# A two-layer decoder trunk in split fp32: new SBUF addresses for h's transpose, the operand sums and the activations

## The chip, the cores and the metric

The kernel runs on one core of one Trainium2 chip. The metric is device time in microseconds (us) of one execution; times of single instructions are in nanoseconds (ns). TensorE does the matrix products (PE in the profile, with PEld for its weight loads), VectorE is DVE, ScalarE is ACT, GpSimd is POOL, and SyncE (SP) issues the DMAs.

## The reference, cut to what matters

Two layers over 512 tokens of width 1024; layer 0 mixes with gated linear attention (GLA), layer 1 with retention. All of it is float32.

```python
for i in range(DEPTH):                       # DEPTH = 2
    h = layer_norm(DN_ALPHA * h + 0.5 * swiglu(h, ffn_w_in[i, 0], ffn_w_out[i, 0]), ...)
    m = gla_mixer(h, ...) if i == 0 else retention_mixer(h, ...)
    h = layer_norm(DN_ALPHA * h + m, ...)
    h = layer_norm(DN_ALPHA * h + 0.5 * swiglu(h, ffn_w_in[i, 1], ffn_w_out[i, 1]), ...)

def swiglu(x, w_in, w_out):                  # 1024 -> 2 x 2816 -> 1024
    gate, up = jnp.split(x @ w_in, 2, axis=-1)
    return (jax.nn.silu(gate) * up) @ w_out
```

## The kernel before

Every float32 operand of a large product is split into a rounded part (`hi`) and the rest (`lo`), both of type fp32r, and one product becomes three matmuls, hi·hi, hi·lo and lo·hi, in `mm3` (L151, L152, L153). A matmul has a *stationary* operand of 128 x 128, which TensorE loads beforehand (LDWEIGHTS, a row of PEld), and a *moving* operand of 256 or 512 columns, which is streamed past it. In the profile's names of matmuls, `out<-a,b`, the moving operand is `a` and the stationary one is `b`: `po<-whi,ahi` streams the weights `whi` past the activation `ahi`.

Weights arrive by DMA in granules of 128 x 2048 floats (`wf`), and ACT and DVE split them into `whi` and `wlo` (L105, L106) ahead of their use. The stages and the roles of the operands are:

- **Feature-major projections** (`fm`): the stationary operand is a block of weights, the moving one is h's transpose `hThi`/`hTlo`, 512 or 256 columns wide.
- **The FFN's first product** (`products`, in `seven_products`): seven half-size products instead of eight. Three of them stream a quarter of hT (`p1`, `a12`, `a22`), four stream a sum of quarters of hT (`Shi`/`Slo`, made once for each FFN in `operand_sums`), each 256 columns wide, with 4 x 3 matmuls to a product. The weights are stationary.
- **The FFN's second product** (`po<-whi,ahi` and so on): a 128-column slice of an activation `ahi`/`alo` is stationary, and 512 columns of weights are streamed. The ten activation buffers of each kind are used in turn.
- **Token-major projections** (`pvr` in GLA, `pv` and `pgg` in retention): a slice of hT is stationary, 512 columns of weights are streamed.
- **The mixers' output product** (`po<-whi,yhi`): a slice of the mixer's result `yhi`/`ylo` is stationary, 512 columns of weights are streamed.

Where a tile lies in SBUF is decided by the order of allocation: each pool is a stack of its tags, one after the other in each partition, each with its size in bytes. `cpool` (h, hT, `ident`, `mhalf`, `wgl`) comes first, then `wpool` (`wf`, `whi`, `wlo`), and above it the pool of the stage (`ffn..`, `gla`, `ret`). Almost all tiles are multiples of 256 bytes long in a partition, so that what stands before a pool decides the address of all of its tiles mod 256. Every slice that a matmul reads begins a multiple of 512 bytes into its tile. So each operand has one address mod 256, whatever the slice:

| operand | mod 256, before |
|---|---|
| `hThi`, `hTlo` | 128 |
| `whi`, `wlo` | 192 |
| `Shi0..3`, `Slo0..3` | 192 |
| `ahi`, `alo` (all) | 192 |
| `yhi`, `ylo` in GLA | 192 |
| `yhi`, `ylo` in retention | 0 |

Of each matmul the text looks at one number, the *distance*: the address of the stationary operand that is loaded for the next matmul, less the address of the moving operand of this matmul, mod 256.

Of the kernel before, what the change touches and what calls it, by code (L numbers as in the profile page):

```python
# [10 lines left out]
F32 = mybir.dt.float32  # L11
F32R = mybir.dt.float32r
# [5 lines left out]
P = 128  # L18
T = 512
# [5 lines left out]
NFC = 10  # L25
# [13 lines left out]
def _ffn_plan():  # L39

    plan = []
    for c, (f0, f1) in enumerate(CHUNKS):
        n = 0
        for f in range(f0, f1):
            plan.append(("in", f))
            if c and (f - f0) % 2 == 0 and n < (CHUNKS[c - 1][1] - CHUNKS[c - 1][0]) // 2:
                plan.append(("out", c - 1, n))
                n += 1  # L50
    return plan + [("out", len(CHUNKS) - 1, i) for i in range((CHUNKS[-1][1] - CHUNKS[-1][0]) // 2)]
# [14 lines left out]
def tile_decoder(ctx: ExitStack, tc: tile.TileContext, a: dict, out: bass.AP):  # L66
    nc = tc.nc
# [3 lines left out]
    cpool = ctx.enter_context(tc.tile_pool(name="cpool", bufs=1))  # L71
# [5 lines left out]
    class Stream:  # L77
# [59 lines left out]
        def next(self):  # L137
            i = self.at
            self.at += 1
            self.prepare(i)  # L140
            self.load(i + 1)
            self.prepare(i + 1)
            self.load(i + 2)
            return self.split[i]
# [10 lines left out]
    def pick(pair, *idx):  # L155
        return tuple(x[idx] for x in pair)
# [4 lines left out]
    def new_hT():  # L161
        hT[0] = tuple(
            cpool.tile([P, KD, T], F32R, tag=f"hT{s}", name=f"hT{s}")
            for s in ("hi", "lo")
        )
        return hT[0]
# [3 lines left out]
    with tc.tile_pool(name="start", bufs=1) as sp:  # L170
        hi, lo = new_hT()
# [13 lines left out]

    ident = cpool.tile([P, P], F32, name="ident")
    make_identity(nc, ident)
    mhalf = cpool.tile([P, 16], F32, name="mhalf")
    nc.gpsimd.memset(mhalf, -0.5)

    wgl = cpool.tile([P, KD, GRANK], F32, name="wgl")
# [1 line left out]
    def load_h():  # L193
        for t in range(NT):
            nc.sync.dma_start(h[t], a["x"][t * P:(t + 1) * P, :])


    def load_gb(tp, n, tags=("ln_g", "ln_b")):
        gb = []
        for name, tag in zip(("ln_g", "ln_b"), tags):  # L200
            x = tp.tile([P, D], F32, tag=tag, name=f"{name}{n}", bufs=1)
            nc.sync.dma_start(x, a[name][n].partition_broadcast(P))
            gb.append(x)
        return gb
# [32 lines left out]
    def feature_major(w, ranges, ps=None):  # L237

        w = [tuple(x.rearrange("p (k c) -> p k c", k=4) for x in b) for b in w]
        ps = ps or [pacc.tile([P, T], F32, tag="acc", name="fm") for _ in range(2)]  # L240
        for j in range(2):
            for r in ranges:
                for k in range(KD):
                    mm3(ps[j][:, r], pick(w[j if k < 4 else 3 - j], slice(None), k % 4),
                        pick(hT[0], slice(None), k, r), k == 0, k == KD - 1)
        return ps

    WHOLE = [slice(0, T)]
    H = T // 2
# [3 lines left out]
    def two_granules_ahead():  # L253


        g = [ws.next(), ws.next()]
        ps = [[pacc.tile([P, T], F32, tag="acc", name="fm") for _ in range(2)] for _ in g]
        for r in HALVES:
            for w, p in zip(g, ps):
                feature_major(w, [r], p)  # L260
        return ps
# [32 lines left out]
    def out_steps(lhs, n, first, halves=(0, 1), tp=None):  # L294


        for half in halves:
            ps = [pacc.tile([P, 512], F32, tag="acc", name="po") for _ in range(NT)]
            for k in range(n):
                def step(r):  # L300
                    for t in range(NT):
                        mm3(ps[t], lhs(k, t), r, k == 0, k == n - 1)
                        if k == n - 1:
                            add_out(t, half, ps[t], first, tp)
                yield step

    def out_by_halves(lhs, n, units, half, first, tp):
        for k, step in enumerate(out_steps(lhs, n, first, [half], tp)):
            step(units[half * n + k])
# [47 lines left out]

    def operand_sums(tp):

        s = [tuple(tp.tile([P, 4, H], F32R, tag=f"S{c}{i}", name=f"S{c}{i}", bufs=1) for c in ("hi", "lo")) for i in range(4)]  # L360
        for c in range(2):
            def full(k, ts, tag):
                x = tp.tile([P, 2, H], F32, tag=tag, name="hsum")
                nc.vector.tensor_add(x, *(y.bitcast(F32) for y in pick(hT[0], slice(None), slice(k + 2 * c, k + 2 * c + 2), ts)))
                return x

            def parts(x, i):
                hi, lo = pick(s[i], slice(None), slice(2 * c, 2 * c + 2))
                nc.scalar.copy(hi, x)
                nc.vector.tensor_sub(lo, x, hi.bitcast(F32))  # L370

            x21 = full(0, HALVES[1], "gate")
            s1 = full(4, HALVES[1], "up")
            nc.vector.tensor_add(s1, s1, x21)
            parts(s1, 0)
            x11 = full(0, HALVES[0], "gate")
            nc.vector.tensor_sub(x21, x11, x21)
            parts(x21, 2)
            nc.vector.tensor_sub(x11, s1, x11)
            parts(x11, 1)  # L380
            x12 = full(4, HALVES[0], "up")
            nc.vector.tensor_sub(x12, x12, x11)
            parts(x12, 3)
        return s

    def ffn(layer, which, ln, last=False, first=False):
        with tc.tile_pool(name=f"ffn{layer}{which}", bufs=2) as tp:
            ws.sums_pool = tp
            act = {}

            def activate(f, gate, up):
                sg = tp.tile([P, T], F32, tag="gate", name="sg")
                nc.scalar.activation(sg, gate, AF.Silu)
                nc.vector.scalar_tensor_tensor(out=sg, in0=sg, scalar=0.5, in1=up, op0=ALU.mult, op1=ALU.mult)
                hi = tp.tile([P, T], F32R, tag="ahi", name="ahi", bufs=NFC)
                lo = tp.tile([P, T], F32R, tag="alo", name="alo", bufs=NFC)
                nc.scalar.copy(hi, sg)
                nc.vector.tensor_sub(lo, sg, hi.bitcast(F32))
                act[f] = (hi, lo)

            def lhs(k0):
                return lambda k, t: tuple(x[:, t * P:(t + 1) * P] for x in act[k0 + k])

            if first:
                for f in range(2):
                    activate(f, *feature_major(ws.next(), WHOLE))
                load_h()
                nc.sync.dma_start(wgl, a["gla_w_low"].rearrange("(k p) c -> p k c", p=P))
            else:
                for f, ps in enumerate(two_granules_ahead()):  # L410
                    activate(f, *ps)
            s = operand_sums(tp)
            outs = {}
            for what, n, *i in _ffn_plan()[2:]:
                f0, f1 = CHUNKS[-1 if what == "in" else n]
                if what == "in":
                    activate(n, *(seven_products(ws.next(), s, tp) if n in FAST else feature_major(ws.next(), WHOLE)))
                elif f1 < NF:
                    if n not in outs:
                        outs[n] = out_steps(lhs(f0), f1 - f0, n == 0)  # L420
                    for u in ws.next():
                        next(outs[n])(u)
            f0, f1 = CHUNKS[-1]
            gb = load_gb(tp, ln, ("Shi0", "Slo0"))
            if not last:
                new_hT()
            def place(j):
                return lambda: tuple(tp.tile([P, 2 * B], F32R, tag=f"S{c}{j}", name=f"w{c}", bufs=1) for c in ("hi", "lo"))

            for j in range(3):  # L430
                ws.place[ws.at + (3 + j) // 2, (3 + j) % 2] = place(1 + j)
            units = Units()
            if not last:
                out_by_halves(lhs(f0), f1 - f0, units, 0, False, tp)
                for i in range(3):
                    ws.prepare(ws.at + i)
            out_by_tokens(lhs(f0), f1 - f0, units, [0, 1] if last else [1], False,
                          lambda t: layer_norm(tp, t, gb, last), tp)
# [200 lines left out]
    def retention(ln):  # L639
        with tc.tile_pool(name="ret", bufs=1) as tp:  # L640
            cos = tp.tile([P, T], F32, name="cos")
            sin = tp.tile([P, T], F32, name="sin")
            gcol = tp.tile([P, 16], F32, name="rgcol")
            for x, n in ((cos, "cos"), (sin, "sin"), (gcol[:, :RDV // P], "ret_norm_g")):
                nc.sync.dma_start(x, a[n])

# [74 lines left out]
            for hd in range(RH):  # L721
# [3 lines left out]
                S = scores(hd, q, k)  # L725
# [13 lines left out]
    ffn(0, 1, 2)  # L739
    ffn(1, 0, 3)  # L740
    retention(4)
    ffn(1, 1, 5, last=True)

# [89 lines left out]
```

## Time and profile before

| | |
|---|---|
| time, median of 3 runs | 2032.46 us (2031.47 to 2032.55) |
| profiled execution, its time | 2032.29 us |
| its span, first to last instruction | 2030.2 us |
| PE busy | 2015.7 us, 99% |
| PEld busy | 1796.5 us, 88% |
| DVE busy | 1515.6 us, 75% |
| ACT busy | 797.2 us, 39% |
| granted TensorE clock | 0.999 |

The busy time of an engine is the union of its instructions' times. A matmul's recorded time reaches beyond the start of the next one, so the *pace*, from one start to the next, is read from the start times. The profiled execution's time is 2.1 us above its span.

### The profile page before, as it was taken

The numbers are of one execution on the slowest core, as the hardware profiler recorded it, in microseconds if no ns is written. First come the engines' busy times: TensorE is split into PE (matmuls) and PEld (weight loads), VectorE is DVE, ScalarE is ACT, GpSimd is POOL, SyncE is SP. The second block draws the span as 40 slices with busy tenths as digits, with TensorE's granted clock in tenths as the row PEclk, the third lists the DMA queues.
The fourth block names the chain that finished last, engine by engine and source line by source line (L and its number), as shares of the span: only waits on it lengthen the run. The fifth ranks groups of instructions, "written<-read, shape, count | busy, mean of one in ns | idle before, by whom it ended". The sixth has DMA issues, their size and how long they took to land.

```text
span 2030.2 us, 29592 instructions
## 1 busy us (share of the span) xinstructions
PE 2015.7 (99%) x12364; PEld 1796.5 (88%) x12364; DVE 1515.6 (75%) x2152; ACT 797.2 (39%) x1131; POOL 37.2 (2%) x56
## 2 busy tenths in 40 slices
PE   8999999999999999999999999999999999999998
PEld 7999998888889999998999998888888878999997
DVE  7888888745588888888888888554545468888886
ACT  5444433632234344443444433333232324443441
POOL 0000000000000000000000000000000000000000
PEclk9999999999999999999999999999999999999999
DMA  6322223112222222341332223222222213322322
GB/s 212 122 104 104 104 95 134 66 66 80 104 83 104 104 104 104 104 146 43 125 104 104 104 88 141 104 76 99 74 91 74 91 69 104 119 91 103 110 98 83
DMA packets 33637, 205.00 MB, mean 101 GB/s; under 512 B 5056, under 2 KB 5184, under 8 KB 10592
## 3 DMA queue, kind: packets, MB, share of 16 engines
q1 hardware_dynamic: 33504, 203.12, 28.2%
q8 instruction: 97, 1.59, 0.3%
q14 instruction: 36, 0.29, 0.0%
HBM read 201.00 MB, written 2.10 MB: 100 GB/s over the span
## 4 chain that ended last, share of the span: by engine, by line
PE 97%; DVE 1%; ACT 1%; DMA 1%; issue 0%; SPq 0%; DVEq 0%; ACTq 0%
PE products L151 12%; PE products L153 12%; PE products L152 12%; PE po L151 10%; PE po L152 10%; PE po L153 10%; PE fm L153 5%; PE fm L151 5%; PE fm L152 5%; PE pv L152 1%; PE pgg L153 1%; PE pv L153 1%; PE pv L151 1%; PE pgg L152 1%; PE pgg L151 1%; PE pvr L153 1%
## 5 line engine op out<-in xcount | busy, mean ns | idle before, releaser
L106 DVE TENSOR_TENSOR wlo<-wf,whi 128x512 fp32r<-128x512 f32 (+1 forms) x362 | 399.4, 1107 | 95.8 <-ACT whi L105 94.3
L105 ACT CAST whi<-wf 128x512 fp32r<-128x512 f32 (+1 forms) x362 | 346.1, 959 | 296.2 <-PE po L153 130.3
L153 PE MATMUL products<-Shi,wlo 128*128 128x256 f32 x1152 | 325.6, 283 | 0.0
L151 PE MATMUL products<-Shi,whi 128*128 128x256 f32 x1152 | 325.5, 283 | 0.0
L152 PE MATMUL products<-Slo,whi 128*128 128x256 f32 x1152 | 324.8, 282 | 0.0
L151 PE MATMUL po<-whi,ahi 128*128 128x512 f32 x704 | 274.9, 391 | 0.0
L152 PE MATMUL po<-wlo,ahi 128*128 128x512 f32 x704 | 274.6, 390 | 0.0
L153 PE MATMUL po<-whi,alo 128*128 128x512 f32 x704 | 274.1, 390 | 0.0
L151 PE MATMUL products<-hThi,whi 128*128 128x256 f32 x864 | 241.1, 279 | 0.0
L152 PE MATMUL products<-hTlo,whi 128*128 128x256 f32 x864 | 240.6, 278 | 0.0
L153 PE MATMUL products<-hThi,wlo 128*128 128x256 f32 x864 | 240.2, 278 | 0.0
L151 PEld LDWEIGHTS products<-Shi,whi 128*128 128x128 f32 x1152 | 219.7, 191 | 0.4
L153 PEld LDWEIGHTS products<-Shi,wlo 128*128 128x128 f32 x1152 | 219.8, 191 | 0.0
L152 PEld LDWEIGHTS products<-Slo,whi 128*128 128x128 f32 x1152 | 219.7, 191 | 0.0
L105 ACT CAST whi<-sums 128x1024 fp32r<-128x1024 f32 x144 | 150.4, 1047 | 158.5 <-DVE h L277 70.1
L151 PE MATMUL fm<-hThi,whi 128*128 128x512 f32 (+1 forms) x592 | 202.0, 341 | 5.1 <-ACT hThi L183 5.1
L152 PE MATMUL fm<-hTlo,whi 128*128 128x512 f32 (+1 forms) x592 | 202.1, 341 | 0.0
L153 PE MATMUL fm<-hThi,wlo 128*128 128x512 f32 (+1 forms) x592 | 201.7, 341 | 0.1
L106 DVE TENSOR_TENSOR wlo<-sums,whi 128x1024 fp32r<-128x1024 f32 x144 | 175.6, 1222 | 24.3 <-ACT whi L105 24.3
L152 PEld LDWEIGHTS products<-hTlo,whi 128*128 128x128 f32 x864 | 162.7, 188 | 1.4
L151 PEld LDWEIGHTS products<-hThi,whi 128*128 128x128 f32 x864 | 162.7, 188 | 1.4
L153 PEld LDWEIGHTS products<-hThi,wlo 128*128 128x128 f32 x864 | 163.5, 189 | 0.0
(185 smaller groups left out, 3423.7 us busy)
## 6 DMA issues: line engine op xcount, KB each, us to landing
wf<-in_wts SPq DMA_DIRECT2D x179, 1024.0 KB, 4.8
ln_b<-in_ln_b SPq DMA_DIRECT2D x6, 512.0 KB, 3.5
ln_g<-in_ln_g SPq DMA_DIRECT2D x6, 512.0 KB, 5.2
xs<-in_xT SPq DMA_DIRECT2D x8, 256.0 KB, 5.3
h<-in_x SPq DMA_DIRECT2D x4, 512.0 KB, 8.1
out_h<-h SPq DMA_DIRECT2D x8, 256.0 KB, 2.0
wf<-in_wts SPq DMA_DIRECT2D x4, 256.0 KB, 5.6
dm<-in_decay SPq DMA_DIRECT2D x4, 256.0 KB, 3.1
```

The source lines that it names most:

```text
L105: nc.scalar.copy(hi, src)
L106: nc.vector.tensor_sub(lo, src, hi.bitcast(F32))
L151: nc.tensor.matmul(ps, l[0], r[0], start=start, stop=False)
L152: nc.tensor.matmul(ps, l[0], r[1], start=False, stop=False)
L153: nc.tensor.matmul(ps, l[1], r[0], start=False, stop=stop)
```

## The change

No instruction is added, taken away or moved on any engine: all five streams hold the same operations on the same tiles in the same order with the same waits. Only the tiles' addresses differ.

```diff
-    mhalf = cpool.tile([P, 16], F32, name="mhalf")
+    mhalf = cpool.tile([P, 32], F32, name="mhalf")
...
-        s = [tuple(tp.tile([P, 4, H], F32R, tag=f"S{c}{i}", name=f"S{c}{i}", bufs=1) for c in ("hi", "lo")) for i in range(4)]
+        s = []
+        for i, n in enumerate((16, 16, 16, 40)):
+            tp.tile([P, n], F32, tag=f"gap{i}", name="gap", bufs=1)
+            s.append(tuple(tp.tile([P, 4, H], F32R, tag=f"S{c}{i}", name=f"S{c}{i}", bufs=1) for c in ("hi", "lo")))
...
-                hi = tp.tile([P, T], F32R, tag="ahi", name="ahi", bufs=NFC)
-                lo = tp.tile([P, T], F32R, tag="alo", name="alo", bufs=NFC)
+                hi, lo = (tp.tile([P, T + 16], F32R, tag=f"a{c}", name=f"a{c}", bufs=NFC)[:, :T] for c in ("hi", "lo"))
...
-            gcol = tp.tile([P, 16], F32, name="rgcol")
+            gcol = tp.tile([P, 64], F32, name="rgcol")
...
-    nc = bacc.Bacc("TRN2", target_bir_lowering=False, num_devices=1)
+    nc = bacc.Bacc("TRN2", target_bir_lowering=False, num_devices=1, dynamic_dma_scratch_size=1024)
```

The last edit frees 15,360 bytes (60 x 256) of each partition at its bottom, which the longer tiles need; it moves everything by a multiple of 256. `mhalf` is 64 bytes longer, so the weights move by 64 against h and hT. Unused tiles of 64, 64, 64 and 160 bytes stand before the four pairs of operand sums. Each activation buffer is 64 bytes longer, so the ten buffers of a kind lie at 0, 64, 128, 192, 0, ... `rgcol` is 192 bytes longer, so what follows it in retention's pool lies at 0 as the weights now do.

The distances, as defined above, with the number of matmuls that have them (fp32r alone; a matmul at the joint of two stages can differ from its group):

| moving, then stationary | columns | matmuls | before | after |
|---|---|---|---|---|
| S, then weights (`products`) | 256 | 3456 | 0 | 192, 128, 64 and 160 for S0, S1, S2 and S3 |
| hT, then weights (`products`, `fm`) | 256 | 3456 | 64 | 128 |
| hT, then weights (`fm`) | 512 | 912 | 64 | 128 |
| weights, then hT (`pvr`, `pv`, `pgg`) | 512 | 1152 | 192 | 128 |
| weights, then activations (`po`) | 512 | 2112 | 0 | 0 for some 541, 64 for 543, 128 for 429, 192 for 460, others for the rest |
| weights, then retention's y (`po`) | 512 | 384 | 64 | 0 |
| weights, then GLA's y (`po`) | 512 | 192 | 0 | 0 |

Inside the mixers (`pS`, `pro`, `pkv`, `pgo`) both operands move together, and their distances stay at 0.

## Rows read from the trace of the kernel before

**Rows 1.** The page: span, busy time and share of each engine, the chain that ended last.

```profile
span 2030.2 us, 29592 instructions
PE 2015.7 (99%) x12364; PEld 1796.5 (88%) x12364; DVE 1515.6 (75%) x2152; ACT 797.2 (39%) x1131; POOL 37.2 (2%) x56
...
PE 97%; DVE 1%; ACT 1%; DMA 1%; issue 0%; SPq 0%; DVEq 0%; ACTq 0%
```

**Rows 2.** Groups by line and shape, PE: columns, count, busy us, mean ns of one.

```profile
L151 PE MATMUL products<-Shi,whi 128*128 128x256 f32 x1152 | 325.5, 283 | 0.0
...
L151 PE MATMUL po<-whi,ahi 128*128 128x512 f32 x704 | 274.9, 391 | 0.0
...
L152 PE MATMUL products<-hTlo,whi 128*128 128x256 f32 x864 | 240.6, 278 | 0.0
...
L152 PE MATMUL fm<-hTlo,whi 128*128 128x256 f32 x288 | 81.0, 281 | 0.0
```

**Rows 3.** Timeline of PE from 679.7 us: start us, duration us, operation.

```profile
679.73 0.28 PE L151 MATMUL products<-Shi,whi 128*128 128x256 f32 x1
...
681.41 0.28 PE L153 MATMUL products<-Shi,wlo 128*128 128x256 f32 x1
681.53 0.29 PE L151 MATMUL products<-hThi,whi 128*128 128x256 f32 x1
...
682.00 0.28 PE L152 MATMUL products<-hTlo,whi 128*128 128x256 f32 x1
...
682.91 0.28 PE L151 MATMUL products<-hThi,whi 128*128 128x256 f32 x1
```

**Rows 4.** The same timeline for PEld, the weight loads.

```profile
681.41 0.19 PEld L151 LDWEIGHTS products<-hThi,whi 128*128 128x128 f32 x1
681.53 0.19 PEld L152 LDWEIGHTS products<-hTlo,whi 128*128 128x128 f32 x1
```

**Rows 5.** Timeline of PE, FFN second product from 70 us.

```profile
70.18 0.39 PE L152 MATMUL po<-wlo,ahi 128*128 128x512 f32 x1
...
73.13 0.39 PE L153 MATMUL po<-whi,alo 128*128 128x512 f32 x1
```

**Rows 6.** Timeline of PE, feature-major projection from 24.6 us.

```profile
24.62 0.39 PE L151 MATMUL fm<-hThi,whi 128*128 128x512 f32 x1
...
36.99 0.40 PE L153 MATMUL fm<-hThi,wlo 128*128 128x512 f32 x1
```

**Rows 7.** Tile yhi, GLA's then retention's window: duration ns minimum/median/maximum, first and last start.

```profile
L151 PE MATMUL po<-whi,yhi x64: 387/389/478, 483.5 to 572.5; 128*128 128x512 f32 x64
L151 PE MATMUL po<-whi,yhi x128: 393/394/501, 1424.9 to 1676.8; 128*128 128x512 f32 x128
```

**Rows 8.** Tile pgg, same columns: matmuls of one token-major projection.

```profile
L151 PE MATMUL pgg<-whi,hThi x128: 388/388/447, 1317.1 to 1619.0; 128*128 128x512 f32 x128
L152 PE MATMUL pgg<-wlo,hThi x128: 391/392/393, 1317.4 to 1619.2; 128*128 128x512 f32 x128
L153 PE MATMUL pgg<-whi,hTlo x128: 393/394/395, 1317.6 to 1619.4; 128*128 128x512 f32 x128
```

**Rows 9.** Tile products, same columns: the fast and the slow operand.

```profile
L151 PE MATMUL products<-Shi,whi x1152: 274/283/388, 55.4 to 1989.3; 128*128 128x256 f32 x192
L153 PE MATMUL products<-hThi,wlo x864: 275/276/282, 52.9 to 1986.5; 128*128 128x256 f32 x173
```

**Rows 10.** Chain that ended last, one long piece: start us, us, what.

```profile
1416.35 0.87 PE ytr L447 x8
```

**Rows 11.** Busy time by stretch (us, count), PE, PEld, DVE, ACT, POOL: third stretch is one FFN.

```profile
600.00:940.00 340.00, 339.90 (x2312) 314.05 (x2311) 280.29 (x386) 140.00 (x193) 3.59 (x4) 1.00 0.29 103
```

**Rows 12.** Waits of PE, the longest: waited for, us in total, times, longest.

```profile
PE fm L151 <- ACT hThi L183: 5.1, 1, 5.1
```

## The prediction

> **What bounds the kernel now.** I read the page first: PE is busy for 99% of the span and holds 97% of the chain that ended last [rows 1]. The waits of PE come next: the longest is one of 5.1 us at the start [rows 12], so nobody makes PE wait, and time can only change where matmuls follow each other faster or slower. The third view is the timeline of PE, for the pace. Eight starts of matmuls of hT at 256 columns take 0.91 us, 114 ns each, and fourteen of S just before take 1.68 us, 120 ns each [rows 3]. At 512 columns thirteen starts of the FFN's second product take 2.95 us, 227 ns [rows 5], and 53 of a projection of hT take 12.37 us, 233 ns [rows 6]. Recorded durations are the pace plus some 163 ns (390 to 227, 283 to 120), so a difference of durations is one of paces, and the tables by shape or tile can be used for whole groups.
>
> The fourth view is the timeline of the weight loads: the load for the next matmul starts with the present matmul, at 681.53 us both [rows 3, 4]. So the operands that are read at the same time are the moving one of this matmul and the stationary one of the next, whose distance the table of the change gives. Does the pace follow it? The best pair is the output product of the mixers: the same code, shape and weights, distance 0 in GLA and 64 in retention, and medians of 389 and 394 ns [rows 7]. At 512 columns the order of paces is then 0 (227), 192 (388, 392 and 394 in turn, on average 391.3, a pace of 228 [rows 8]), 64 (231 to 233). At 256 columns it is the other way round: distance 0 gives a median of 283, distance 64 one of 276 [rows 9]. So the effect is real, about 6 ns for a matmul, but its sign depends on the width, and the distances 128 and 160, to which the change takes most matmuls, occur in no row, nor 192 at 256 columns.
>
> **The change part by part.** It removes and adds no instruction and no wait, so each term is a count of matmuls times a difference of durations.
>
> *Operand sums, 3456 matmuls of 256 columns, from distance 0 to 192, 128, 64 and 160.* Now 325.5 us / 1152 = 282.6 ns each; hT in the same function at distance 64 takes 240.6 / 864 = 278.5 [rows 2] (three rows of each kind, alike). A quarter goes to 64, for which the row of hT stands: 864 x -4.1 = -3.5 us. For the other three quarters I know only that they leave 0, the slow case at this width. Bounds: 276, the fast median [rows 9], which gives 2592 x -6.6 = -17.1, and no gain at all, 0. One more step of 6 ns upwards isn't excluded by a row either (+15.6), but no group of 256 columns shows it. I take the mean of hT for these too, -4.1 x 2592 = -10.6, since only distance 0 is seen to be slow. Sum of the term -14.1.
>
> *hT at 256 columns, 3456 matmuls, from 64 to 128.* Now 278.5 in `products` (2592) and 281 in `fm` (864) [rows 2]. Bounds: all at the fast median of 276, 2592 x -2.5 + 864 x -5 = -10.8 us; all at 283, the pace of distance 0, 2592 x 4.5 + 864 x 2 = +13.4. I take 0, between the ends.
>
> *hT at 512 columns, 912 matmuls, from 64 to 128.* Pace 233 now [rows 6]; bounds 227 [rows 5] and 233: -5.5 to 0. The three known distances give 227, 228, 233, so I take the middle, 230: -2.7.
>
> *Weights past hT, 1152 matmuls, from 192 to 128.* Now 391.3; bounds 389 and 394 [rows 7, 8]: -2.6 to +3.1. I take 0.
>
> *Activations, 2112 matmuls, at 0 now with 391 on average [rows 2] and a pace of 227 [rows 5].* 543 go to 64, +5 ns [rows 7]: +2.7. 460 go to 192, +2.3 [rows 8]: +1.1. 429 to 128 and some 90 to others, for which I take the middle of 0 and 5: +1.3. Sum +5.1, bounds +3.8 and +6.4.
>
> *Retention's y, 384 matmuls, from 64 to 0:* -5 ns each [rows 7], -1.9. GLA's y stays.
>
> Sum: -14.1 + 0 - 2.7 + 0 + 5.1 - 1.9 = -13.6 us. The profiled execution takes 2032.3 us (span 2030.2 and 2.1 around it), which is 0.2 below the median of the runs shown; so the change would end near 2019 us, and I round to 2020, since a few matmuls at joints keep neither pace.
>
> What covers this: an FFN is 340 us with DVE busy for 280 [rows 11], and it sheds 3 us or so, to 83% for DVE. The splitting of weights stays ahead. Were that cover gone, PE would wait for `wlo`, and the gain would stop there; 280 in 337 leaves far more than that. DMA moves what it moved. The shorter descriptor scratch concerns no transfer here, since all of this kernel's are issued by SP in hardware queues.
>
> A page of the notes speaks against all this. The Trainium skill, page "TensorE: Matmul & The Clock Gate", section Part 2 (step 1), says that TensorE reads its moving operand and its weights through two independent ports, so that loading the next weights takes nothing from the running matmul; "SBUF — State Buffer", section Who interferes with whom, adds that PE waits on nobody. By that rule addresses would cost nothing and the time would stay at 2032. The rows on the two mixers' output products, 389 against 394, don't agree with it.
>
> **The rivals.**
>
> *Half a period is the bad distance for hT (slower).* All 3456 matmuls of hT at 256 columns move to 128, and 1728 of the sums to 128 and 160 or thereabouts. If what makes 64 fast at this width is special to 64, the 128 is as slow as 0: +13.4 for hT, -3.5 for the one operand sum that gets 64, 0 for the other three, +3.1 for the weights past hT, 0 for hT at 512, +6.4 and -1.9: +17.5, 2050 us. For it: of the distances seen at 256 columns just one is fast, and at 512 the best distance is the slow one of 256, so the paces don't simply grow or fall with distance. Against it: hT at 64 isn't at its fast pace throughout (mean 278.5 and 281, median 276), so 64 isn't clean itself. It decides from a mean of hT at 128 above some 282 ns.
>
> *All that leaves 0 and 64 becomes fast.* Then the sums run at 276 (864 x -6.6 - 17.1 = -22.8), hT gives -10.8, at 512 columns 128 is as good as 0 (-5.5 and -2.6), activations +3.8, retention's y -1.9: -39.8, 1993 us. For it: a weight load of 128 columns can follow the last one every 109 ns (8 transposes in 0.87 us [rows 10]), so the pace of 113 isn't even the floor. Against: it wants the best case five times over; half of it, some -25 us or 2007, is likelier.
>
> *Distance doesn't matter; the operand does.* S at 120 and hT at 114 could differ by what DVE and ACT do meanwhile, since sums are streamed when their drains run. Then nothing moves but the 384 of retention, and the time stays within 4 us of 2032. Against it stands the pair of [rows 7], where the distance is all that differs.
>
> **How the numbers follow.** The forecast, faster by some 8 to 20 us, gets 0.45; the larger gain 0.15; the slower rival 0.25; no change, by that rival or because terms cancel, 0.15. A measurement of this kernel can tell a change of about 0.2% (4 us) from none. So faster 0.59 (with all of the first two but a hundredth), same 0.15, slower 0.26. The likeliest case alone is 2012 to 2025. The range for 8 in 10 reaches into both other cases: down to 2000, which leaves out the lower third of the large gain, and up to 2048, just below the full price of the slower rival.
>
> **What would show it.** PE keeps 12364 matmuls and no wait above 5 us. The groups `products<-S..` fall from 283 to about 278; if only a quarter falls, the medians by tile stay at 283. `products<-hT..` tells the sign: below 279 for a gain, at 283 for the slower rival. `fm` at 512 columns goes to a pace of 227 to 233; retention's `po<-whi,yhi` to a median of 389, which tests distance alone; `po<-whi,ahi` rises from 391 to about 393. The prediction is wrong if 128 costs hT more than 2 ns a matmul, or if a distance that no row shows has a pace outside 113 to 120 at 256 columns or 227 to 233 at 512.

## The result, and the profile after

The changed kernel takes 2049.4 us (median of 4 runs, 2048.7 to 2050.3) against 2032.2 us (4 runs, 2031.5 to 2032.6): a ratio of 1.0081, with a 95% interval of 1.0069 to 1.0094. It is slower by 17 us where I forecast faster by 12, and it ends 1.4 us outside the range.

The page of the changed kernel answers to [rows 1]: span, busy time, and the chain that ended last.

```profile
span 2046.6 us, 29592 instructions
...
PE 2032.9 (99%) x12364; PEld 1805.0 (88%) x12364; DVE 1517.0 (74%) x2152; ACT 795.1 (39%) x1131; POOL 37.2 (2%) x56
...
PE 98%; DVE 1%; ACT 1%; DMA 0%; issue 0%; DVEq 0%; ACTq 0%
```

The counts are the same, DVE and ACT are where they were, and PE alone is 17.2 us busier. Its longest wait is the one of [rows 12], unchanged. So the premise held: the matmuls follow each other more slowly, and nothing else happened. The groups by line and shape say which (count | busy us, mean ns of one), against [rows 2]:

```profile
L151 PE MATMUL products<-Shi,whi 128*128 128x256 f32 x1152 | 324.2, 282 | 0.0
L152 PE MATMUL products<-Slo,whi 128*128 128x256 f32 x1152 | 323.2, 281 | 0.0
L153 PE MATMUL products<-Shi,wlo 128*128 128x256 f32 x1152 | 322.6, 280 | 0.0
...
L151 PE MATMUL po<-whi,ahi 128*128 128x512 f32 x704 | 277.5, 394 | 0.0
...
L152 PE MATMUL products<-hTlo,whi 128*128 128x256 f32 x864 | 243.3, 282 | 0.0
...
L152 PE MATMUL fm<-hTlo,whi 128*128 128x512 f32 x304 | 120.9, 398 | 0.0
L152 PE MATMUL fm<-hTlo,whi 128*128 128x256 f32 x288 | 81.8, 284 | 0.0
```

S falls by 1 to 3 ns (325.5 to 324.2 us in its first row) where 4 were forecast. hT at 256 columns rises by 3 in both of its groups, and the activations by 4 to 5 (the row shown, by 3.7, is the least of their three). In the view of tile `products` (ns minimum/median/maximum, first to last start) the fast operand of [rows 9] is no longer fast:

```profile
L151 PE MATMUL products<-Shi,whi x1152: 276/281/392, 55.2 to 2005.0; 128*128 128x256 f32 x192
...
L153 PE MATMUL products<-hThi,wlo x864: 274/281/287, 52.6 to 2002.3; 128*128 128x256 f32 x173
```

hT's median goes from 276 to 281, up to the slow operand beside it. The same view of tile `yhi`, in retention's window, has the one edit that was priced from a pair of rows, and it came as priced, from 394 [rows 7] to 389:

```profile
L151 PE MATMUL po<-whi,yhi x128: 388/389/499, 1439.1 to 1689.3; 128*128 128x512 f32 x128
```

Tile `pgg` has weights past hT, which in [rows 8] took 388, 392 and 394 in turn at distance 192. At 128 all three take 393:

```profile
L151 PE MATMUL pgg<-whi,hThi x128: 390/393/445, 1330.4 to 1632.4; 128*128 128x512 f32 x128
L152 PE MATMUL pgg<-wlo,hThi x128: 390/393/404, 1330.6 to 1632.7; 128*128 128x512 f32 x128
L153 PE MATMUL pgg<-whi,hTlo x128: 389/393/404, 1330.9 to 1632.9; 128*128 128x512 f32 x128
```

All terms of the prediction, measured in one execution of either kernel (us): the busy time of each group's rows before and after, its change, and, beside it, the change of the time from each matmul's start to the next one's:

| term | before | after | measured | start to start | predicted |
|---|---|---|---|---|---|
| operand sums | 975.9 | 970.0 | -5.9 | -4.1 | -14.1 |
| hT at 256 columns | 964.2 | 975.1 | +10.9 | +11.0 | 0 |
| hT at 512 columns | 363.5 | 363.2 | -0.3 | -0.5 | -2.7 |
| weights past hT | 453.2 | 455.1 | +1.9 | +3.0 | 0 |
| activations | 823.6 | 833.0 | +9.4 | +9.9 | +5.1 |
| mixers' y | 227.4 | 225.4 | -2.0 | -2.2 | -1.9 |
| sum | | | +14.0 | +17.0 | -13.6 |

The span grew by 16.4. The durations leave 2.4 us of it out; the start times have it all, since the matmuls outside these groups come to -0.7. So a difference of durations is not quite one of paces: the sums at distance 0 last 163 ns longer than their pace (283.2 against 120.0), those at 192 only 161.5 (279.3 against 117.8).

### The profile page after: what moved, and what is told of

The parts are those of the page before. It is cut to its first block, busy times and chain, and to the rows that moved or that the text cites. A ratio compares the mean times of both kernels' runs of the same rounds, so it can differ in the third digit from the quotient of the medians.

```text
span 2046.6 us, 29592 instructions
## 1 busy us (share of the span) xinstructions
PE 2032.9 (99%) x12364; PEld 1805.0 (88%) x12364; DVE 1517.0 (74%) x2152; ACT 795.1 (39%) x1131; POOL 37.2 (2%) x56
## 4 chain that ended last, share of the span: by engine, by line
PE 98%; DVE 1%; ACT 1%; DMA 0%; issue 0%; DVEq 0%; ACTq 0%
PE products L151 12%; PE products L152 12%; PE products L153 12%; PE po L152 10%; PE po L153 10%; PE po L151 10%; PE fm L151 5%; PE fm L152 5%; PE fm L153 5%; PE pgg L151 1%; PE pv L153 1%; PE pv L151 1%; PE pv L152 1%; PE pgg L153 1%; PE pgg L152 1%; PE pvr L151 1%
## 5 line engine op out<-in xcount | busy, mean ns | idle before, releaser
L151 PE MATMUL products<-Shi,whi 128*128 128x256 f32 x1152 | 324.2, 282 | 0.0
L153 PE MATMUL po<-whi,alo 128*128 128x512 f32 x704 | 277.7, 395 | 0.0
```

Source lines behind the costliest of these rows:

```text
L151: nc.tensor.matmul(ps, l[0], r[0], start=start, stop=False)
L153: nc.tensor.matmul(ps, l[1], r[0], start=False, stop=stop)
```

## The experiments

The theory after the result: distance 128 is slow for hT at 256 columns, and that alone makes the change slower. The rivals: the lost time comes from the operand sums or the activations, or from the parts acting on each other. Four kernels make one part of the change each. All experiments are shown as edits of the kernel before, but for one that edits the changed kernel; all but the first also have the shorter descriptor scratch of the change.

**hT alone at 128.** This also takes weights past hT to 128, as the change does.

```diff
-    mhalf = cpool.tile([P, 16], F32, name="mhalf")
+    mhalf = cpool.tile([P, 32], F32, name="mhalf")
```

> Only the weights' distance to hT is changed, 64 to 128; the sums, activations and y keep their distances. Theory A (half a period is the bad distance for hT, and the parts add up): the products of hT at 256 columns go from 278.5 to about 282 ns, the token-major ones from 391 to about 395, in all 10 to 17 us slower, 2042 to 2049. Theory B (the loss comes from the activations, which are moved to mixed distances, and from what that does to their neighbours): within 5 us of 2032.

Measured: 2048.3 against 2032.4, ratio 1.0077 (1.0061 to 1.0094), +15.8 us. Sixteen floats more in one small tile cost nearly what the whole change costs. Two groups by line, and the last row of hT in tile `products`, of this kernel:

```profile
L152 PE MATMUL products<-hTlo,whi 128*128 128x256 f32 x864 | 243.8, 282 | 0.0
...
L152 PE MATMUL fm<-hTlo,whi 128*128 128x256 f32 x288 | 82.1, 285 | 0.0
```

```profile
L153 PE MATMUL products<-hThi,wlo x864: 279/282/285, 53.0 to 2002.5; 128*128 128x256 f32 x173
```

From a median of 276 to 282, with S untouched at 283; the mean of 243.8 us / 864 = 282.2 ns is past the 282 from which the rival was to hold.

From start to start hT at 256 columns has +11.9 us of this, and the weights past hT +4.8. Some 1.6 of the 4.8 are the clock: from 376.7 to 379.9 us the granted clock of this execution is 0.50 (the lower level, 1.2 GHz), behind GLA's gate products `pz`, and eight matmuls of `pvr` follow each other every 427 ns. Eight of the thirteen traces of the experiments have such a stretch there, of 3.4 or 6.8 us, and those of before and after have none; executions of the kernel before went from a median of 2031.8 us at a mean granted clock of 0.999 to 2034.8 at 0.997. So up to 3 us in a single execution says nothing of an edit.

The kernel also shows that the distance counts and not the address itself: all that lies above `mhalf` moved by 64 bytes, and S, the activations and y, whose distances stayed, kept their paces (119.7, 227.8 and 234.1 ns on average, before 119.4, 227.8 and 234.0).

**The operand sums alone**, with the change's unused tiles before them.

```diff
-        s = [tuple(tp.tile([P, 4, H], F32R, tag=f"S{c}{i}", name=f"S{c}{i}", bufs=1) for c in ("hi", "lo")) for i in range(4)]
+        s = []
+        for i, n in enumerate((16, 16, 16, 40)):
+            if n:
+                tp.tile([P, n], F32, tag=f"gap{i}", name="gap", bufs=1)
+            s.append(tuple(tp.tile([P, 4, H], F32R, tag=f"S{c}{i}", name=f"S{c}{i}", bufs=1) for c in ("hi", "lo")))
```

> Only the four gaps before the operand sums. Both theories: the sums go from 282.5 to about 280.5 ns, 3456 x 2 = 7 us faster, 2025; if the matmuls of hT between them change too although their distance stays at 64, distance alone doesn't set the pace, but also what ran before.

Measured: 2027.8, ratio 0.9976 (0.9967 to 0.9986), -4.7 us. The sums at 64, 128, 160 and 192 take 277.7, 282.2, 281.9 and 279.8 ns on average, so only half of them leave the slow pace. hT, at its old 64, is at 277.6.

**The activations alone.**

```diff
-                hi = tp.tile([P, T], F32R, tag="ahi", name="ahi", bufs=NFC)
-                lo = tp.tile([P, T], F32R, tag="alo", name="alo", bufs=NFC)
+                hi, lo = (tp.tile([P, T + 16], F32R, tag=f"a{c}", name=f"a{c}", bufs=NFC)[:, :T] for c in ("hi", "lo"))
```

> Only the longer activation buffers. If each matmul is paid by its own distance, the quarter that stays at 0 keeps 227 ns and the whole gives 5 us, 2037. If hi and lo, which now lie 128 apart, disturb one another inside the three matmuls, all quarters get slower, 391 to about 394.5 on average, 9 us, 2041.

Measured: 2039.9, ratio 1.0036 (1.0022 to 1.0049), +7.5 us. Even the activations at distance 0 take 394.2 ns here on average, where all took 390 before.

**Retention's y alone.**

```diff
-            gcol = tp.tile([P, 16], F32, name="rgcol")
+            gcol = tp.tile([P, 64], F32, name="rgcol")
```

> Only retention's column of factors is longer, so that its y lies at distance 0, and the smaller descriptor scratch. Distance rules: the 384 matmuls of retention's output product go from a median of 394 to 389, 2 us faster, and nothing else moves by a microsecond, so this is also the control for the scratch.

Measured: 2030.4, ratio 0.9990 (0.9980 to 0.9999), -2.0 us. No other group moves by more than 1.0 us from start to start, so the shorter scratch is not seen to cost anything. The size is that of the count times 5 ns; by itself it is less than a measurement can tell from none, and the row of tile `yhi` carries it:

```profile
L151 PE MATMUL po<-whi,yhi x128: 387/389/499, 1424.9 to 1674.6; 128*128 128x512 f32 x128
```

The four parts add up to 15.8 - 4.7 + 7.5 - 2.0 = +16.6, beside +17.3 for the whole. So the parts nearly add up, and the first rival falls too: the sums gain. The activations are a second loss beside hT.

**Why do activations at distance 0 get slower?** Among the changed buffers `ahi` and `alo` of one chunk lie 128 apart, so the three matmuls of `mm3` alternate between distances. Two kernels part this from the distance itself. In the first, hi and lo rotate together, always at one distance:

```diff
+        for i, n in enumerate((32, 0, 0, 0)):
...
+                hi = tp.tile([P, T + 16], F32R, tag="ahi", name="ahi", bufs=NFC)[:, :T]
+                if not act:
+                    tp.tile([P, 32], F32, tag="gapa", name="gap", bufs=1)
+                lo = tp.tile([P, T + 16], F32R, tag="alo", name="alo", bufs=NFC)[:, :T]
```

> The buffers still take turns at 0, 64, 128, 192, but lo lies where hi lies. If each matmul pays for its own distance: 389 at 0, 391 at 192, about 393 at 128 and 394 at 64, in the mean some 391.5, 3 us slower than before, 2035. If the turn from one buffer to the next is what costs, it stays near 394.5, 2040.

Measured: 2038.9, ratio 1.0030 (1.0019 to 1.0041), +6.0 us; medians 390, 395, 393 and 392 ns at 0, 64, 128 and 192. The medians are what the prediction had assumed; the means are up to 2 ns above them. Part of that is the way from one distance to the next: of the twelve matmuls on a buffer at 0, behind one at another distance, the first take 393 to 395 ns on average and only the seventh 390.

In the second nothing rotates: all of hi at 0, all of lo at 128.

```diff
+        for i, n in enumerate((32, 0, 0, 0)):
...
+                if not act:
+                    tp.tile([P, 32], F32, tag="gapa", name="gap", bufs=1)
```

> No turns: all hi at 0, all lo at 128. If the mixture inside the three matmuls of a product costs, also the matmuls at distance 0 go to 393 to 395, 8 to 10 us slower, 2041. If each pays for its own distance, two in three keep 389 and the third goes to about 393, 3 us, 2035.

Measured: 2040.9, ratio 1.0039 (1.0024 to 1.0054), +7.9 us. Its tiles `ahi` and `alo`:

```profile
L151 PE MATMUL po<-whi,ahi x704: 388/390/484, 62.9 to 2030.1; 128*128 128x512 f32 x176
L152 PE MATMUL po<-wlo,ahi x704: 387/397/483, 63.2 to 2030.3; 128*128 128x512 f32 x176
L153 PE MATMUL po<-whi,alo x704: 390/397/487, 63.4 to 2030.5; 128*128 128x512 f32 x176
```

The first matmul runs while the second load of `ahi` comes from distance 0, and takes 390. The second runs beside the load of `alo` at 128: 397. The third runs beside the next `ahi`, at distance 0 again, and still takes 397. So mixing costs a matmul that has the good distance itself. That both the own distance and the mixing cost is shown; how the 9.4 us of the changed kernel divide between them is not, since hi and lo together at one distance is dearer by the durations (394.0 ns on average against 390) than its medians say.

**Is 64 a good distance for the sums too?** All of them at 64, like hT:

```diff
+        for i, n in enumerate((48, 0, 0, 0)):
```

> All four operand sums at distance 64, as hT. If 64 is the good distance at 256 columns for every operand: from 282.5 to 277, 3456 x 5.5 = 19 us faster, less some 2 us for weights that lie in the sums' place, 2015. If the sums are slow for another reason: unchanged, 2032.

Measured: 2031.8, ratio 0.9996 (0.9986 to 1.0005): nothing, and not the gain of some 20 us that 276 ns for all 3456 would have brought. Tile `products`:

```profile
L151 PE MATMUL products<-Shi,whi x1152: 275/282/395, 55.4 to 1989.3; 128*128 128x256 f32 x192
...
L153 PE MATMUL products<-hThi,wlo x864: 275/282/282, 52.9 to 1986.6; 128*128 128x256 f32 x173
```

hT was not touched, has its old distance, and went from 276 to 282. The distance alone no longer says the pace. The timeline of PE (start us, duration us) behind one of the FFN's second products:

```profile
72.91 0.39 PE L153 MATMUL po<-whi,alo 128*128 128x512 f32 x1
73.14 0.28 PE L151 MATMUL products<-hThi,whi 128*128 128x256 f32 x1
...
75.96 0.28 PE L151 MATMUL products<-Shi,whi 128*128 128x256 f32 x1
...
78.79 0.28 PE L151 MATMUL products<-hThi,whi 128*128 128x256 f32 x1
...
83.03 0.28 PE L151 MATMUL products<-hThi,whi 128*128 128x256 f32 x1
...
85.86 0.28 PE L151 MATMUL products<-Shi,whi 128*128 128x256 f32 x1
```

24 matmuls lie between the first and the second start of `products`, 24 to the third, 36 to the fourth and 24 to the fifth: 118 ns each throughout, hT and S alike, 12.7 us long. In the kernel before, hT at the same distance ran at 114 behind a stretch of S at 0 [rows 3]. So the new theory was: distance 64 has two paces, 113 and 118. It takes the slow one behind the 512-column product and keeps it; a stretch at distance 0, slow itself, gives back the fast one. It is not the only thing that does: in three of the four FFNs of this kernel two matmuls of the last products were held up by some 170 ns together (in the first FFN 185 and 223 ns from start to start, at 314.6 us), and what followed, still at 64, ran at 113.

**Sums in turn at 64 and 0**, so that a stretch at 0 comes between stretches at 64:

```diff
+        for i, n in enumerate((48, 16, 48, 16)):
```

> S0 and S2 at distance 64, S1 and S3 left at 0, so that a stretch at 0 stands ahead of each stretch at 64. If the pace at 64 depends on what ran before (fast after a stretch at 0, slow after itself): S0, S2 and hT at 276 to 277, S1 and S3 at 283, so 1728 x 6 + 2592 x 1.5 = 14 us faster less 1 for displaced weights, 2019. If each matmul pays by its own distance with the means of the kernel with all sums at 64 (281.3 for sums and hT at 64): 1728 x 1 us less, 2592 x 2.8 more, 5 us slower, 2037.

Measured: 2021.0, ratio 0.9943 (0.9928 to 0.9958), -11.2 us. S0 and S2, at 64, have a median of 276; S1 and S3, at 0, one of 282; hT is back at 276. It is the fastest kernel so far.

**Sums at 192, with one at 64 and none at 0:**

```diff
+        for i, n in enumerate((16, 0, 32, 32)):
```

> S2 at 64 and the other three at 192, the cheapest distances of the kernel with the sums alone. By its rows (279.8 at 192, 277.7 at 64, hT 277.6): 2592 x 2.7 + 864 x 4.7 + 2592 x 0.9 = 13 us faster, less 1 for displaced weights, 2020. If the stretches at 128 and 160 were what made the others fast there, no better than that kernel: 2028.

Measured: 2033.9, ratio 1.0007 (0.9998 to 1.0017): no gain. hT's row in tile `products`:

```profile
L153 PE MATMUL products<-hThi,wlo x864: 276/281/281, 53.3 to 1990.3; 128*128 128x256 f32 x173
```

192 runs at 118 and does not give back the fast pace: S2 at 64 (280.4 ns) and hT at 64 (280.7) stay slow, with nothing at 0 before them.

**hT at 192 and at 0**, for the rest of the table of distances.

```diff
-    mhalf = cpool.tile([P, 16], F32, name="mhalf")
+    mhalf = cpool.tile([P, 48], F32, name="mhalf")
```

> hT at 192 instead of 64 at both widths, the token-major products at 64 instead of 192. By the sums at 192 (279.7): 1.5 ns more for 3456 matmuls, 5 us; at 512 columns 2 ns less for 912 and 1 ns more for 1152. In all 3 to 6 us slower, 2037. If 64 is the only good distance at 256 columns, 282 as at 128: 13 us slower, 2045.

Measured: 2044.5, ratio 1.0058 (1.0041 to 1.0075), +11.6 us. hT in `products` has a median of 279, as S does at 192. Weights past hT, now at 64, cost 5.2 us, and `fm` at 512 columns gains 2.5. By durations the groups make some 8 of the 11.6; from start to start they make 12.9, and with -0.4 in the other matmuls that is the whole growth of the span. The difference is mostly hT in `products`, which goes from 115.6 to 118.0 ns and loses 6.2 us, where its durations say 2.5. Some 2.4 of the 12.9, in `pvr`, are a stretch at the lower clock (0.50 from 374.3 to 380.9 us). The time is that of the second expectation, but not for its reason, 282 ns as at 128.

```diff
+    mhalf = cpool.tile([P, 64], F32, name="mhalf")
```

> hT at 0 at both widths and with the weights past it. At 256 columns 283 as the sums at 0, 3456 x 4.2 = 14 us slower; at 512 columns 389 for 912 + 1152 matmuls, 9 us faster; together 2037. If 64 is needed for the fast pace of all products, sums included, 2045 and more.

Measured: 2040.9, ratio 1.0042 (1.0025 to 1.0059), +8.7 us. Groups by line of this kernel:

```profile
L152 PE MATMUL products<-hTlo,whi 128*128 128x256 f32 x864 | 244.5, 283 | 0.0
...
L152 PE MATMUL fm<-hTlo,whi 128*128 128x512 f32 x304 | 119.5, 393 | 0.0
...
L152 PE MATMUL pv<-wlo,hThi 128*128 128x512 f32 x128 | 49.8, 389 | 0.0
```

With hT at 0 it has the 283 of S at 0, so hT and S are alike and the rival "The operand does" falls. At 512 columns the same address gains: 393 for 398 in `fm`, 389 for 396 in `pv`. The widths want opposite things.

**The changed kernel with hT back at 64:**

```diff
-    mhalf = cpool.tile([P, 32], F32, name="mhalf")
+    mhalf = cpool.tile([P, 16], F32, name="mhalf")
```

> The whole change but for the 64 bytes between hT and the weights, so hT stays at 64. If the loss is hT at 128 and the parts add up: 2049.4 less 15.8, 2033.6, within 2 us. If the parts act on one another: off by more than 4 us.

Measured: 2031.2, ratio to before 0.9995 (0.9986 to 1.0004). Taking back this one part returns 18.3 us, all of the 17.3 that were lost. That is 2.4 less than the sum of the parts had it. Here the parts do act on each other: behind six of the eight pieces of an FFN's second product, whose activations no longer lie at 0, hT starts at 115 or 116 ns, not 118 (as in the kernel with the activations alone), and `products<-hT..` gain 3.6 us from start to start against before, with hT at 64 in both. The time is no better than before: with hT left alone, the change would have gained nothing clear of noise.

**One stretch at 0, the rest at 64.** If one stretch at 0 is enough to give back the fast pace, only S1 needs to lie there; retention's y goes to 0 as in the change.

```diff
+        for i, n in enumerate((48, 16, 48, 0)):
...
+            gcol = tp.tile([P, 64], F32, name="rgcol")
```

> S1 alone at distance 0, the other three sums and hT at 64, and retention's y at 0. If a stretch at 0 brings the pace at 64 back from 118 to 113 ns and the fast pace then lasts until the next product of the FFN's second half: all products but S1, and but those of hT between such a product and S1, at 276 to 277; S3 gains 864 x 5.5 = 5 us over the kernel with S1 and S3 at 0, y another 2: 2014. If one stretch at 0 isn't enough for a granule, the later products go back to 281: 2025 and more.

Measured in 5 runs: 2015.1 (2014.8 to 2017.2) against 2032.3, ratio 0.9918 (0.9904 to 0.9932): 17 us faster than before and 34 faster than the changed kernel. Its page, tile `products`, and the timeline of PE at the same place as above:

```profile
span 2013.1 us, 29592 instructions
...
PE 1999.4 (99%) x12364; PEld 1780.9 (88%) x12364; DVE 1515.6 (75%) x2152; ACT 798.7 (40%) x1131; POOL 37.2 (2%) x56
```

```profile
L151 PE MATMUL products<-Shi,whi x1152: 276/276/387, 55.8 to 1971.8; 128*128 128x256 f32 x192
...
L153 PE MATMUL products<-hThi,wlo x864: 276/276/281, 53.2 to 1969.0; 128*128 128x256 f32 x173
```

```profile
73.61 0.28 PE L151 MATMUL products<-hThi,whi 128*128 128x256 f32 x1
...
76.43 0.28 PE L151 MATMUL products<-Shi,whi 128*128 128x256 f32 x1
...
77.87 0.29 PE L151 MATMUL products<-Shi,whi 128*128 128x256 f32 x1
...
79.25 0.28 PE L151 MATMUL products<-hThi,whi 128*128 128x256 f32 x1
...
84.69 0.28 PE L151 MATMUL products<-hThi,whi 128*128 128x256 f32 x1
```

The first 24 matmuls, hT at 64 behind the 512-column product, take 2.82 us, 118 ns each. Then comes S1 at 0, 12 matmuls in 1.44 us, 120 each. S2 at 64 follows: 12 in 1.38 us, 115 with the joint at its start. After it 48 matmuls of hT and S at 64 take 5.44 us, 113 each.

## Why the prediction was wrong

**What bounds the kernel: right.** PE kept its count and its waits, and PE's busy time took the whole difference. Nothing was uncovered on DVE.

**The step that failed: hT at 256 columns, "I take 0, between the ends".** It measured +10.9 us, close to its upper end of +13.4: 3.2 ns for each of the 2592 in `products` and 3.0 for each of the 864 in `fm`, more than the 2 that the prediction named as a sign of being wrong. The run with hT alone at 128 shows it as the cause, and the changed kernel with hT back at 64 shows how far it goes: it makes the change slower instead of even, while the gain that was forecast was lost in the sums and the activations, 8.2 and 4.3 us short of their terms. The slow rival, "Half a period is the bad distance for hT", named this place, this sign and the threshold of 282 ns, and had 0.25. A middle between two ends was the wrong choice here, because it was no estimate: of the two distances known at 256 columns one was fast, and it was the one being left. Moving hT could hardly gain: already at a median of 276, it had 2.5 ns to win and 4.5 to lose.

**Operand sums, -14.1: right in sign, too large.** Measured -5.9. "Only distance 0 is seen to be slow" was true of the rows and not of the distances: 128 and 160 take 282 ns, like 0, and 192 takes 280. Only S2 and S0 gained. And the quarter at 64 did not get the 278.5 of hT's row: behind hT and S1 at 128 it averaged 279.7.

**Activations, +5.1: right in sign, too small.** Measured +9.4. The prices of single distances stood up (medians 390, 395, 393, 392 with hi and lo together). What was missing is that a triple with hi and lo at different distances pays in matmuls that lie well themselves (390 to 397), and that the average lies above the median even without that.

**The rest.** hT at 512 columns went from a median pace of 233 to 232, not 230 (-0.3 for -2.7); weights past hT came to +1.9, inside the bounds of -2.6 to +3.1, though they were priced by `pgg` alone; retention's y is right to 0.1 us. "Pace plus some 163 ns" is good to 2 ns a matmul, which is as much as some of the differences that it was to price. The rival's total of 2050 beside the measured 2049.4 is partly luck: it had hT too dear by 2.5 us, the weights past hT by 1.2 and the gain of the sums too small by 2.4, which nearly offset the activations (3.0 more than it had) and the 2.4 that the durations leave out.

**The rule of two independent ports**, from the Trainium skill, page "TensorE: Matmul & The Clock Gate", section Part 2 (step 1), by which the time would have stayed at 2032, doesn't agree with these runs: the weights, moved by 64 bytes against hT with every instruction the same and no wait longer, cost 15.8 us, of which the clock has some 1.6 in the profiled execution.

## What to carry to other kernels

In a kernel that TensorE holds for 99% of its span, the addresses mod 256 bytes of the moving operand and of the next weights are worth some 0.8% either way, and 64 bytes more in one small tile can spend all of it. Move one operand at a time, weighing each width by its count, since the address that helps 512 columns hurt 256 here. A group's median at a given distance is a price only for the order in which it was read: check what ran before it, and leave an operand that already has its fast median where it is.

## What the runs showed of the hardware that I had not expected

Paces from start to start in ns, by distance, for fp32r matmuls with a fresh weight load each, at a granted clock of 1.00 (from the start times, in whole stretches):

| distance | 256 columns | 512 columns |
|---|---|---|
| 0 | 118 to 120 | 227 |
| 64 | 113 or 118 | 231 to 236 |
| 128, 160 | 118 to 120 | 228 to 241, 233 on average (128 alone) |
| 192 | 118 | 226 to 232, 229 on average, in `pgg`; in parts of `pv` and `pvr` 233 |

At 256 columns, distance 64 holds one of two paces. Entered from the FFN's second product with all activations at 0 it runs at 118 through stretches at 64 and 192, until a stretch at 0, or in one kernel a pause of some 170 ns, ends it; then it runs at 113 until the next such product. So in the kernel before, the slow sums at 0 were what kept hT fast. A stretch at 128 ended it in the kernel with the sums alone, but not in the changed kernel, where S2 at 64 ran at 118 behind hT and S1 at 128 in every second set of the seven products. And with the activations at other distances hT often starts at 115 behind the second product. This is a relation of paces to addresses and order, seen in the kernels above; what in the chip makes it was not found, nor why the second product leaves the slow pace behind. At 512 columns the third matmul of a triple that mixes distances keeps the slow 397 although its own load lies at 0, which may be of the same kind, but that was not tested.
